# Three convolution tiles moved to TensorE column quarters, and attention's value products turned round

## The chip, the cores and the metric

The kernel runs on one core of one Trainium2 chip. The metric is device time in microseconds, as the median of several executions. One execution was also profiled, and all rows below are of that one.

## The reference, cut to what matters

Two networks follow each other; only the first one (two layers, 512 tokens and 16 meta tokens, so L = 528 rows of width 1024) is touched by the change. Per layer, in float32:

```python
proj = h @ w_in[l]                       # a, g, zc, q, k, v, za, qi, ki, wi
u = a * sigmoid(g)                       # 512 channels
u[t, c] = sum_j w_dw[j, c] * u[t - 30 + j, c] + b_dw[c]     # 31 taps, depthwise
y_conv = silu(layer_norm(u)) * silu(zc)
score = sum_h relu(qi_h . ki) * wi_h     # index scores, causal
keep the 132 best keys per query (top-k)
s = q . k / 8 on the kept keys, 8 heads of 64
p = softmax(s); y_attn = (p @ v) * silu(za)
h = layer_norm(4 ** 0.25 * h + concat(y_conv, y_attn) @ w_out[l])
```

The second network (windowed attention, a gated linear attention, 16 experts, a final gate) starts when the first has ended.

## The kernel before, in words

Activations lie transposed, with channels on the 128 partitions and the 528 (first layer) or 512 (second layer) rows along the free axis. A projection tile (`proj`, the products on L181) makes 128 output channels in 48 recorded passes: eight slices of the contraction, three products of high and low parts (`wh`, `wl`, `hTh`, `hTl`), two pieces of 264 columns. Its weights come in `raw` tiles (three buffers), are split by ScalarE (L159) and VectorE (L160), and its result lies in a PSUM tile of the tag `pp`, which has two buffers.

`p_ag(c)` makes 128 convolution channels: the projections a and g, a tanh (L339), and the product `u` (L340). Then `conv_tap` runs 31 taps over it. For the channel groups in `pconv` (0, 1 and 2 in the first layer, 0 and 1 in the second) ScalarE multiplies by the tap (L323) and GpSimd adds (L325). For the others, group 3 in the first layer and groups 2 and 3 in the second, VectorE does a multiply and add for each tap (L328 and L330). The three tiles of the title are these.

`attn(i)` handles 128 queries: products of queries and keys (L252, L258, two heads at a time in the two row halves of the array), scores plus mask on VectorE into a tile `smb` (L585), the exponential on ScalarE (L590), transposes of the probabilities (L558), copies to SBUF (`pT`, L561), and the value products (L565) with the transposed probabilities as the stationary operand and 64 value columns as the moving one. The rows of a block are then divided by their sums (L505 to L507). In the tail of the layer each block is transposed again (L500) and multiplied by the gate `sza` (L501), and the output projection follows (`pp<-yah,wh` on L181).

The order of issue on each engine is fixed at compile time from priorities, written down as `self.plan`. In the first layer the levels run w, topk, tail, idx, proj, conv, att, ag, rest, fill; in the second w, tail, idx, conv, proj, att, ag, topk, rest, fill. The phases are traced in these orders:

```python
('ag0', 'idx', 'q', 'k', 'sc', 'v', 'ag2', 'ag3', 'topk', 'ag1', 'zc', 'att', 'za')   # first layer
('idx', 'q', 'k', 'sc', 'ag1', 'v', 'ag0', 'ag3', 'topk', 'ag2', 'att', 'za', 'zc')   # second layer
```

A tile is allocated by tag: all tiles of a tag share its buffers (`sb(shape, name, tag, bufs)`). The tag `sm` has two buffers; before the change only `smb` and the gated result in the tail (`yah`, `yal`) use it in the first network. The PSUM tag `s` with four buffers holds every PSUM tile that isn't `pp`. DMAs of weights, and those of `vM` (16 partitions each, from SBUF to SBUF, L481), are issued from SyncE's queue (SPq).

Of the kernel before, what the change touches and what calls it, by code (L numbers as in the profile page):

```python
# [24 lines left out]
W31 = 31  # L25
PAD = W31 - 1
ALPHA = 4.0 ** 0.25
# [41 lines left out]
class Net:  # L69
# [202 lines left out]
    def layer(self, l):  # L272
# [25 lines left out]
        nc.vector.tensor_copy(cvec, pcv)  # L298
        taps = self.sb([128, 4, 31], "taps")
        nc.vector.tensor_scalar(taps, cvec[:, :, 0:31], 0.5, None, op0=ALU.mult)  # L300

# [15 lines left out]
        def conv_tap(c, j):  # L317
            src = u[:, c, j + q0:j + q0 + T]
            if c in pconv:
                if not prod:  # L320
                    prod.append(self.sb([128, 2, L], "prod", "zM"))
                pr = prod[0][:, j % 2, :T] if j else cv[:, c, :]
                nc.scalar.activation(pr, src, AF.Identity, scale=taps[:, c, j:j + 1], bias=0.0 if j else cvec[:, c, 31:32])  # L323
                if j:
                    nc.gpsimd.tensor_tensor(cv[:, c, :], cv[:, c, :], pr, op=ALU.add)  # L325
                return
            if j == 0:
                nc.vector.tensor_scalar(cv[:, c, :], src, taps[:, c, 0:1], cvec[:, c, 31:32], op0=ALU.mult, op1=ALU.add)  # L328
            else:
                nc.vector.scalar_tensor_tensor(cv[:, c, :], src, taps[:, c, j:j + 1], cv[:, c, :], op0=ALU.mult, op1=ALU.add)  # L330

        def p_ag(c):
            self.go("ag")
            ps = []
            for n in ("a", "g"):
                raw = self.load_w(w_in, WCOL[n] + 128 * c, 128)
                ps.append(self.proj(self.split_w(raw), 128, hT, KT, fsegs))
            th = self.sb([128, L], "th", "rl", 3)
            nc.scalar.activation(fseg(th), ps[1], AF.Tanh, scale=0.5)  # L339
            nc.vector.scalar_tensor_tensor(fseg(u[:, c, PAD:]), fseg(th), 1.0, ps[0], op0=ALU.add, op1=ALU.mult)  # L340
            self.go("conv")
            for j in range(W31):
                conv_tap(c, j)
# [75 lines left out]
        def topk_short(i):  # L419
# [5 lines left out]
            m8 = self.sb([128, 8], "m8", bufs=4)  # L425
            v = self.sb([128, 1], "tkv")
            pad = -out % 8
# [64 lines left out]
        def gated(col, r, src):  # L492

            if not gate_ready:
                rows_out.append((col, r, src))
                return
            sza = gate_ready[0]
            pt = self.ps([128, 4, 128], "tp")
            for k in range(4):
                nc.tensor.transpose(pt[:, k, :r], src[:r, k * 128:(k + 1) * 128], self.ident[:r, :r])  # L500
            nc.vector.tensor_mul(sza[:, :, col:col + r], pt[:, :, :r], sza[:, :, col:col + r])  # L501
# [32 lines left out]
        def attn(i):  # L534
# [15 lines left out]
            mxv = mx.rearrange("p (x q) -> p q x", q=2)  # L550
            po = self.ps([128, 8, 64], "po")
            first = [True]

            def pv(p, x0, sm):
                pt = self.ps([128, 4, 128], "tp")
                for x in range(hb):
                    for j in range(i + 1):
                        nc.tensor.transpose(pt[:, x * (i + 1) + j, :], sm[:, x, 128 * j:128 * (j + 1)], self.ident)  # L558
                n = hb * (i + 1)
                pT = self.sb([128, 4, 128], "pT", bufs=4)  # L560
                nc.scalar.copy(pT[:, :n], pt[:, :n])  # L561
                for x in range(hb):
                    h = 2 * (x0 + x) + p
                    for j in range(i + 1):
                        nc.tensor.matmul(po[:, h, :], pT[:, x * (i + 1) + j, :], v[:, j, h * 64:(h + 1) * 64], start=first[0],  # L565
                                         stop=False, skip_group_check=True)
                        first[0] = False

            pend = []
            for x0 in range(0, 4, hb):  # L570
# [4 lines left out]
                for x in range(hb):  # L575
                    for p in (1, 0):
                        b = slice(64 * p, 64 * p + 64)
                        pairs.append(((pss[p][:, x, :], qT[b, x0 + x, qc], kT[b, x0 + x, NM:w]), dict(start=True, stop=True)))
                self.burst(pairs, pss[0][0:1, 0, 0:1])
                for p in range(2):  # L580
                    xs = slice(x0, x0 + hb)
# [6 lines left out]
                    for x in range(hb):  # L588
                        h = 2 * (x0 + x) + p
                        nc.scalar.activation(sm[:, x, :], sm[:, x, :], AF.Exp, bias=mx[:, h:h + 1], scale=0.125,  # L590
                                             accum_out=ssum[:, h:h + 1])
                    pend.append((p, x0, sm))
                yield
                while len(pend) > 2:
                    pv(*pend.pop(0))
# [11 lines left out]
            nc.scalar.copy(pT, pt)  # L607
            nc.tensor.matmul(po.rearrange("p h d -> p (h d)"), pT, vM, start=False, stop=True, skip_group_check=True)
            dst = yas[i // 2][:, i % 2, :]
            normalise(po, ssum, 128, dst)  # L610
            gated(col, 128, dst)
            yield

# [1061 lines left out]
    def first_block(self):  # L1675
# [12 lines left out]
        for i in range(4):  # L1688
            self.transposes_to(*self.hT, NM + 128 * i, z[:, i, :])
        for l in range(2):  # L1690
            self.cur = None
            self.layer(l)
# [26 lines left out]
```

## Time and profile before

| | us |
|---|---|
| median of 3 executions | 1849.26 |
| lowest and highest | 1848.18, 1853.11 |
| the profiled execution, its time | 1850.64 |
| its span in the profile | 1848.8 |
| mean granted TensorE clock | 0.965 |

The profiled execution's time is 1.84 us above its span and 1.38 us above the median. The first layer ends near 400 us, the second near 760; the rest belongs to the second network. The clock is given as a share of 2.4 GHz.

### The profile page before, as it was taken

How to read it: one execution, taken by the hardware profiler on the slowest of the kernel's cores; microseconds unless marked ns; L12 is line 12 of the kernel's file. 1: busy time of each engine (PE TensorE's matmuls, PEld its weight loads, DVE VectorE, ACT ScalarE, POOL GpSimd, SP SyncE). 2: the span in 40 equal slices, each digit the busy share in tenths (PEclk: the TensorE clock that was granted, in tenths of full speed). 3: DMA queues.
4: the chain of work that ended last, by engine and by line, in shares of the span. 5: the costliest groups of instructions: out<-in, count | busy, mean ns of one | idle time of the engine just before them, and what ended most of it. 6: DMA issues, size and time to landing. Idle time of an engine off the chain costs nothing.

```text
span 1848.8 us, 27815 instructions
## 1 busy us (share of the span) xinstructions
PE 1686.7 (91%) x11323; PEld 1342.3 (73%) x11323; DVE 1010.8 (55%) x1947; ACT 765.4 (41%) x1310; POOL 238.0 (13%) x161
## 2 busy tenths in 40 slices
PE   6989989889998899799999999999899988888888
PEld 6989877889997789799888899999533332233246
DVE  3899994666998985775533445543401221012044
ACT  3874656447666554634355444322300000000026
POOL 1620863000068400000000000000000000000000
PEclk9999989999999899899989999999999999999999
DMA  6213111121222112222122248556799999999961
GB/s 194 69 47 93 46 46 46 30 70 59 69 61 79 46 47 81 89 69 91 36 63 75 76 143 288 158 211 230 280 421 421 421 420 421 421 420 421 419 273 46
DMA packets 147104, 323.35 MB, mean 175 GB/s; under 512 B 13034, under 2 KB 102826, under 8 KB 128672
## 3 DMA queue, kind: packets, MB, share of 16 engines
q1 hardware_dynamic: 142112, 310.54, 45.3%
q10 hardware_dynamic: 3856, 7.37, 1.1%
q0 software_dynamic: 1008, 3.67, 0.5%
q8 instruction: 89, 1.46, 0.3%
q14 instruction: 39, 0.32, 0.1%
HBM read 305.22 MB, written 16.25 MB: 174 GB/s over the span
## 4 chain that ended last, share of the span: by engine, by line
PE 58%; DMA 17%; DVE 15%; ACT 6%; issue 3%; POOL 1%; SPq 0%; ACTq 0%; DVEq 0%; POOLq 0%
PE pp L181 36%; PE pp L1571 7%; DMA rawe<-in_w_exp_down 7%; DMA rawe<-in_w_exp_gate 4%; DMA rawe<-in_w_exp_up 4%; DVE cv L330 3%; PE pp L1631 2%; DVE wl L160 2%; POOL cv L325 1%; ACT wh L159 1%; DVE smb L585 1%; PE po L565 1%; DVE acc L414 1%; DMA rawe<-in_w_ple_gate 1%; DVE m L413 1%
## 5 line engine op out<-in xcount | busy, mean ns | idle before, releaser
L325 POOL TENSOR_TENSOR cv<-cv,prod 128x528 f32<-128x528 f32 (+1 forms) x150 | 231.1, 1541 | 393.7 <-ACT prod L323 385.0
L1571 PE MATMUL pp<-rawe,xf 128*64 128x512 f32 x1024 | 247.8, 600 | 12.7 <-DMA rawe<-in_w_exp_gate 8.6
L181 PE MATMUL pp<-hTh,wh 128*128 128x264 f32 (+2 forms) x1056 | 227.4, 296 | 22.9 <-ACT th L339 8.0
L159 ACT CAST wh<-raw 128x1024 fp32r<-128x1024 f32 (+2 forms) x149 | 150.9, 1016 | 229.7 <-PE pp L181 204.0
L181 PE MATMUL pp<-hTl,wh 128*128 128x264 f32 (+2 forms) x1056 | 226.9, 295 | 0.1
L181 PE MATMUL pp<-hTh,wl 128*128 128x264 f32 (+2 forms) x1056 | 224.6, 293 | 0.0
L160 DVE TENSOR_TENSOR wl<-raw,wh 128x1024 fp32r<-128x1024 f32 (+2 forms) x149 | 187.5, 1259 | 65.9 <-ACT wh L159 59.2
L181 PEld LDWEIGHTS pp<-hTh,wh 128*128 128x128 f32 (+1 forms) x1056 | 170.9, 195 | 29.7 <-ACT th L339 9.3
L1571 PEld LDWEIGHTS pp<-rawe,xf 128*64 128x64 f32 x1024 | 76.8, 137 | 158.5 <-issue 131.0
L181 PEld LDWEIGHTS pp<-hTl,wh 128*128 128x128 f32 (+1 forms) x1056 | 170.7, 195 | 7.5 <-issue 6.7
L181 PEld LDWEIGHTS pp<-hTh,wl 128*128 128x128 f32 (+1 forms) x1056 | 169.8, 194 | 2.2 <-issue 1.6
L181 PE MATMUL pp<-xTh,wh 128*128 128x264 f32 (+1 forms) x752 | 156.3, 289 | 2.8 <-ACT op L1000 2.3
L181 PE MATMUL pp<-xTl,wh 128*128 128x264 f32 (+1 forms) x752 | 156.5, 288 | 0.5 <-DVE xTl L1095 0.5
L181 PE MATMUL pp<-xTh,wl 128*128 128x264 f32 (+1 forms) x752 | 155.2, 286 | 0.0
L1571 PE MATMUL pp<-rawe,hid 128*64 128x512 f32 x512 | 127.6, 616 | 18.6 <-DMA rawe<-in_w_exp_down 18.1
L1460 DVE SCALAR_TENSOR_TENSOR Y<-pp,per,Y 128x512 fp32r<-128x512 f32 x16 | 12.0, 749 | 232.7 <-ACT Y L1459 232.7
L1428 POOL DMA_INDIRECT xr<-xrows,slots x7 | 6.7, 958 | 993.2 <-DMA xrows<-zr 699.5
L323 ACT ACTIVATE prod<-u,taps 128x528 f32<-128x528 f32 (+1 forms) x150 | 107.6, 729 | 50.4 <-POOL cv L325 50.0
L181 PEld LDWEIGHTS pp<-xTh,wh 128*128 128x128 f32 (+1 forms) x752 | 116.8, 190 | 4.8 <-ACT op L1000 2.5
L181 PEld LDWEIGHTS pp<-xTl,wh 128*128 128x128 f32 (+1 forms) x752 | 116.2, 189 | 3.1 <-issue 2.2
L181 PEld LDWEIGHTS pp<-xTh,wl 128*128 128x128 f32 (+1 forms) x752 | 116.1, 189 | 0.8 <-issue 0.8
L1571 PEld LDWEIGHTS pp<-rawe,hid 128*64 128x64 f32 x512 | 40.6, 141 | 99.5 <-issue 61.0
(504 smaller groups left out, 2972.1 us busy)
## 6 DMA issues: line engine op xcount, KB each, us to landing
rawe<-in_w_exp_gate SPq DMA_DIRECT2D x53, 1024.0 KB, 16.3
rawe<-in_w_exp_up SPq DMA_DIRECT2D x52, 1024.0 KB, 15.0
rawe<-in_w_exp_down SPq DMA_DIRECT2D x51, 1024.0 KB, 19.6
raw<-in_w_in SPq DMA_DIRECT2D x45, 1024.0 KB, 5.3
rawe<-in_w_exp_down SPq DMA_DIRECT2D x26, 512.0 KB, 15.5
rawe<-in_w_exp_up SPq DMA_DIRECT2D x22, 512.0 KB, 16.2
rawe<-in_w_exp_gate SPq DMA_DIRECT2D x22, 512.0 KB, 17.4
raw<-in_w_in SPq DMA_DIRECT2D x20, 512.0 KB, 6.5
```

The lines of the kernel that those rows point to most:

```text
L159: nc.scalar.copy(wh, raw_view)
L160: nc.vector.tensor_sub(wl, raw_view, wh.bitcast(F32))
L181: nc.tensor.matmul(ps[:m, s, x:min(x + k, n)], a[:, t, :m], b[:, c0 + x:min(c0 + x + k, c1)], start=(t == 0 and pi == 0 and x == 0), stop= ...
L323: nc.scalar.activation(pr, src, AF.Identity, scale=taps[:, c, j:j + 1], bias=0.0 if j else cvec[:, c, 31:32])
L325: nc.gpsimd.tensor_tensor(cv[:, c, :], cv[:, c, :], pr, op=ALU.add)
L330: nc.vector.scalar_tensor_tensor(cv[:, c, :], src, taps[:, c, j:j + 1], cv[:, c, :], op0=ALU.mult, op1=ALU.add)
L413: nc.vector.max(m8, acc)
L414: nc.vector.match_replace(acc, m8, acc, NEG_MARK)
L565: nc.tensor.matmul(po[:, h, :], pT[:, x * (i + 1) + j, :], v[:, j, h * 64:(h + 1) * 64], start=first[0], stop=False, skip_group_check=True)
L585: nc.vector.tensor_tensor_reduce(sm[:, x, :], pss[p][:, x, :], acc[:, NM:w], 1.0, mi[:, h:h + 1], ALU.add, ALU.max, mx[:, h:h + 1])
L1571: nc.tensor.matmul(ps[a, s, :], x[:, a], r, start=(t == 0 and k == 0), stop=(t == KT - 2 and k == 1), skip_group_check=True)
L1631: nc.tensor.matmul(ps[k][:, k, :], a[:, t, :], wp[t][:, w, k * 512:(k + 1) * 512], start=(t == 0 and pi == 0), stop=(t == KT - 1 and pi == 2))
```

## The change

- `taps` gets a leading zero, so that there are 32 taps, and `u` one more column of padding.
- `conv_products(c)` replaces VectorE's taps for the three tiles. Sixteen small products with slices of the identity spread the taps over PSUM, and one VectorE product with `mask32` makes of them 32 diagonal blocks `w` (128 x 32 each). Sixteen DMAs on SyncE's queue copy `u`, 32 channels at a time and shifted by 0 to 3 rows, into two tiles `us` of the tag `sm`. Then 64 products, eight for each of four channel quarters and two halves of the rows, put 32 output channels each on one column quarter of the array, and ScalarE copies the sum with the bias to `cv`.
- In `attn`, the value products have the values as the stationary operand (64 columns, on one column half of the array for each of two heads) and the probabilities as the moving one, so that the result `po` is transposed. The reciprocal sums are brought to that layout by eight products with a broadcast column (`pr`), a ScalarE copy and a VectorE product. The gate is then one VectorE product, without transposes. The product with the meta values `vM` becomes four.
- `mask32` is made once at the start.

```diff
-PAD = W31 - 1
+PAD = W31
+CQ = 4
...
-        taps = self.sb([128, 4, 31], "taps")
-        nc.vector.tensor_scalar(taps, cvec[:, :, 0:31], 0.5, None, op0=ALU.mult)
+        taps = self.sb([128, 4, W31 + 1], "taps")
+        nc.vector.memset(taps[:, :, 0:1], 0.0)
+        nc.vector.tensor_scalar(taps[:, :, 1:], cvec[:, :, 0:31], 0.5, None, op0=ALU.mult)
...
-            if j == 0:
-                nc.vector.tensor_scalar(cv[:, c, :], src, taps[:, c, 0:1], cvec[:, c, 31:32], op0=ALU.mult, op1=ALU.add)
-            else:
-                nc.vector.scalar_tensor_tensor(cv[:, c, :], src, taps[:, c, j:j + 1], cv[:, c, :], op0=ALU.mult, op1=ALU.add)
...
+        def conv_products(c):
+            n = T // 2
+            nx = T + W31 + 1 - CQ
+            pt = self.ps([128, 4, 8], "pcv")
+            for g in range(4):
+                for k in range(CQ):
+                    nc.tensor.matmul(pt[32 * k:32 * k + 32, g, :], self.ident[:, 32 * g:32 * g + 32], taps[:, c, k::CQ], start=True, stop=True)
+            w = self.sb([128, 4, 8, 32], "cwt", "k2l")
+            nc.vector.tensor_tensor(w.rearrange("p g e c -> p (g e) c"), self.mask32[:, None, :].to_broadcast([128, 32, 32]),
+                                    pt.rearrange("p g e -> p (g e)")[:, :, None].to_broadcast([128, 32, 32]), op=ALU.mult)
+            us = [self.sb([128, 2, nx], "us", "sm", 2) for _ in range(2)]
+            for g in range(4):
+                for k in range(CQ):
+                    nc.sync.dma_start(us[g // 2][32 * k:32 * k + 32, g % 2, :], u[32 * g:32 * g + 32, c, k + q0:k + q0 + nx])
+            ps = self.ps([128, 2, 512], "pp", "pp", 2)
+            for k in range(2):
+                products = []
+                for e in range(8):
+                    for g in (3, 2, 1, 0):
+                        x0 = CQ * e + n * k
+                        products.append(((ps[32 * g:32 * g + 32, k, :n], w[:, g, e, :], us[g // 2][:, g % 2, x0:x0 + n]),
+                                         dict(start=e == 0, stop=e == 7, skip_group_check=True)))
+                self.burst(products)
+            nc.scalar.activation(cv[:, c, :].rearrange("p (k n) -> p k n", k=2), ps[:, :, :n], AF.Identity, scale=1.0, bias=cvec[:, c, 31:32])
...
+            if c not in pconv:
+                conv_products(c)
+                return
...
-            po = self.ps([128, 8, 64], "po")
+            po = self.ps([128, 4, 128], "po")
...
+                products = []
                 for x in range(hb):
                     for j in range(i + 1):
-                        nc.tensor.matmul(po[:, h, :], pT[:, x * (i + 1) + j, :], v[:, j, h * 64:(h + 1) * 64], start=first[0],
-                                         stop=False, skip_group_check=True)
+                        for p in (1, 0):
+                            h = 2 * (x0 + x) + p
+                            products.append(((po[64 * p:64 * p + 64, x0 + x, :], v[:, j, h * 64:(h + 1) * 64], pTs[p][:, x * (i + 1) + j, :]),
+                                             dict(start=first[p], stop=False, skip_group_check=True)))
+                self.burst(products)
...
-            nc.tensor.matmul(po.rearrange("p h d -> p (h d)"), pT, vM, start=False, stop=True, skip_group_check=True)
+            for x in range(4):
+                nc.tensor.matmul(po[:, x, :], vM[:, 128 * x:128 * x + 128], pT, start=False, stop=True, skip_group_check=True)
+            rs = self.sb([128, 8], "rs", bufs=2)
+            nc.vector.reciprocal(rs, ssum)
+            nc.vector.tensor_scalar(rs, rs, 0.5, None, op0=ALU.mult)
+            pr = self.ps([128, 4, 128], "tp")
+            self.burst([((pr[64 * (h % 2):64 * (h % 2) + 64, h // 2, :], rs[:, h:h + 1].to_broadcast([128, 64]), self.ident),
+                         dict(start=h < 2, stop=True, skip_group_check=True)) for h in range(8)])
             dst = yas[i // 2][:, i % 2, :]
-            normalise(po, ssum, 128, dst)
-            gated(col, 128, dst)
+            nc.scalar.copy(dst, pr.rearrange("p x q -> p (x q)"))
+            nc.vector.tensor_mul(dst, dst, po.rearrange("p x q -> p (x q)"))
+            gated(col, None, dst)
```

`gated(col, None, dst)` multiplies `dst` into the gate without transposes. `burst` issues its products one behind the other on TensorE.

## Rows read from the trace of the kernel before

**Rows 1.** The page: busy time by engine, and the chain that ended last by line.
```profile
PE 1686.7 (91%) x11323; PEld 1342.3 (73%) x11323; DVE 1010.8 (55%) x1947; ACT 765.4 (41%) x1310; POOL 238.0 (13%) x161
...
PE pp L181 36%; PE pp L1571 7%; DMA rawe<-in_w_exp_down 7%; DMA rawe<-in_w_exp_gate 4%; DMA rawe<-in_w_exp_up 4%; DVE cv L330 3%; PE pp L1631 2%; DVE wl L160 2%; POOL cv L325 1%; ACT wh L159 1%; DVE smb L585 1%; PE po L565 1%; DVE acc L414 1%; DMA rawe<-in_w_ple_gate 1%; DVE m L413 1%
```

**Rows 2.** Stretches: us; busy PE, PEld, DVE, ACT, POOL; PEclk; DMA share; GB/s.
```profile
185.00:327.00 142.00, 127.54 (x908) 113.98 (x908) 113.33 (x248) 90.95 (x181) 89.83 (x58) 0.93 0.14 45
549.00:695.00 146.00, 131.64 (x982) 118.89 (x981) 132.40 (x288) 86.14 (x172) 64.73 (x43) 0.94 0.18 57
...
620.00:630.00 10.00, 5.22 (x29) 4.18 (x28) 10.00 (x20) 1.45 (x2) 4.95 (x4) 0.68 0.00 0
640.00:650.00 10.00, 10.00 (x81) 9.04 (x81) 9.93 (x27) 3.47 (x6) 0.00 (x0) 1.00 0.00 0
```

**Rows 3.** Groups of instructions by form up to 780 us: busy us, mean ns.
```profile
L330 DVE SCALAR_TENSOR_TENSOR cv<-u,taps,cv 128x512 f32<-128x512 f32 x60 | 54.9, 927 | 0.5
L330 DVE SCALAR_TENSOR_TENSOR cv<-u,taps,cv 128x528 f32<-128x528 f32 x30 | 34.7, 1157 | 0.2
```

**Rows 4.** TensorE's groups, 185 to 327 and 549 to 695 us; chain, one tile.
```profile
L181 PE MATMUL pp<-hTl,wh 128*128 128x264 f32 x184 | 41.9, 309 | 0.0
L565 PE MATMUL po<-v,pT 128*128 128x64 f32 x160 | 21.3, 277 | 3.9 <-ACT pT L561 3.9
L558 PE MATMUL tp<-base,smb 128*128 128x128 f32 x80 | 12.3, 277 | 1.1 <-ACT smb L590 0.8
...
L181 PE MATMUL pp<-hTh,wl 128*128 128x264 f32 x204 | 44.8, 297 | 0.0
...
148.90 5.88 PE pp L181 x48
```

**Rows 5.** TensorE in order of time: start, us, line, count.
```profile
196.72 0.50 PE L558 MATMUL tp<-base,smb 128*128 128x128 f32 x3
197.15 0.59 PE L252 MATMUL pidx<-qk 64*128 64x384 f32 x1
...
293.76 1.02 PE L608 MATMUL po<-vM,pT 128*128 128x512 f32 x2
...
681.30 0.72 PE L565 MATMUL po<-v,pT 128*128 128x64 f32 x5
681.86 0.28 PE L605 MATMUL tp<-base,smm 128*128 128x128 f32 x1
...
682.35 0.49 PE L655 MATMUL tp<-base,cv 128*128 128x128 f32 x3
...
1401.50 1.51 PE L1571 MATMUL pp<-rawe,xf 128*64 128x512 f32 x6
```

**Rows 6.** ScalarE and VectorE in order of time: convolution read, products `u`.
```profile
673.40 0.20 ACT L650 ACTIVATE warm<-cv 128x1 f32<-128x1 f32 x1 [3.79 <-DVE cv L330]
...
200.72 0.69 DVE L340 SCALAR_TENSOR_TENSOR u<-th,pp 128x528 f32<-128x528 f32 x1
...
587.60 0.73 DVE L340 SCALAR_TENSOR_TENSOR u<-th,pp 128x528 f32<-128x528 f32 x1
...
615.85 0.69 DVE L340 SCALAR_TENSOR_TENSOR u<-th,pp 128x528 f32<-128x528 f32 x1
```

**Rows 7.** Tiles `smb` and `vM`: duration ns min/median/max, first and last start.
```profile
L585 DVE CUSTOM_DVE_ANT_0 smb<-pidx,acc,mi x64: 339/536/751, 185.2 to 675.1; 128x384 f32<-128x384 f32 x16, 128x128 f32<-128x128 f32 x16, 128x256 f32<-128x256 f32 x16, 128x512 f32<-128x512 f32 x16
...
L481 SPq DMA_DIRECT2D vM<-vm x16: 507/576/625, 148.8 to 548.0; - x16
...
DMA to landing us min/median/max: 1.8/2.2/3.4
```

**Rows 8.** The end of the first layer's attention, and SyncE's queue, in order of time.
```profile
326.67 0.67 DVE L507 TENSOR_TENSOR yas<-po,rs 128x512 f32<-128x512 f32 x1
...
333.12 0.82 PE L181 MATMUL pp<-yah,wh 128*128 128x264 f32 x3 [2.59 <-ACT yah L195]
...
532.57 0.38 SPq L151 DMA_DIRECT2D raw<-in_w_in  x1
```

More of the change, by code (lines that the diff above doesn't have):

```diff
@@ L317, in conv_tap @@
         def conv_tap(c, j):
[L318 to L326, printed above, removed]
@@ L327, in conv_tap @@
-            if j == 0:
-                nc.vector.tensor_scalar(cv[:, c, :], src, taps[:, c, 0:1], cvec[:, c, 31:32], op0=ALU.mult, op1=ALU.add)
-            else:
-                nc.vector.scalar_tensor_tensor(cv[:, c, :], src, taps[:, c, j:j + 1], cv[:, c, :], op0=ALU.mult, op1=ALU.add)
+            src = u[:, c, j + 1 + q0:j + 1 + q0 + T]
+            if not prod:
+                prod.append(self.sb([128, 2, L], "prod", "zM"))
+            pr = prod[0][:, j % 2, :T] if j else cv[:, c, :]
+            nc.scalar.activation(pr, src, AF.Identity, scale=taps[:, c, j + 1:j + 2], bias=0.0 if j else cvec[:, c, 31:32])
@@ new lines, in conv_tap @@
+            if j:
+                nc.gpsimd.tensor_tensor(cv[:, c, :], cv[:, c, :], pr, op=ALU.add)
+        def conv_products(c):
[22 more added lines that the diff above has]
+            nc.scalar.activation(cv[:, c, :].rearrange("p (k n) -> p k n", k=2), ps[:, :, :n], AF.Identity, scale=1.0, bias=cvec[:, c, 31:32])
@@ L425, in topk_short @@
             m8 = self.sb([128, 8], "m8", bufs=4)
-            v = self.sb([128, 1], "tkv")
+            v = self.sb([128, 1], "tkv", "am")
             pad = -out % 8
@@ L497, in gated @@
             sza = gate_ready[0]
+            if r is None:
+                dst = sza[:, :, col:col + 128]
+                nc.vector.tensor_mul(dst, src.rearrange("p (x q) -> p x q", x=4), dst)
+                return
             pt = self.ps([128, 4, 128], "tp")
@@ L550, in attn, with pv @@
             mxv = mx.rearrange("p (x q) -> p q x", q=2)
-            po = self.ps([128, 8, 64], "po")
-            first = [True]
-            def pv(p, x0, sm):
-                pt = self.ps([128, 4, 128], "tp")
+            po = self.ps([128, 4, 128], "po")
+            first = [True, True]
+            def pv(x0, sms):
+                n = hb * (i + 1)
+                pTs = []
+                for p in range(2):
+                    pt = self.ps([128, 4, 128], "tp")
+                    for x in range(hb):
+                        for j in range(i + 1):
+                            nc.tensor.transpose(pt[:, x * (i + 1) + j, :], sms[p][:, x, 128 * j:128 * (j + 1)], self.ident)
+                    pTs.append(self.sb([128, 4, 128], "pT", bufs=4))
+                    nc.scalar.copy(pTs[p][:, :n], pt[:, :n])
+                products = []
                 for x in range(hb):
                     for j in range(i + 1):
[L558 to L564, printed above, removed]
-                        nc.tensor.matmul(po[:, h, :], pT[:, x * (i + 1) + j, :], v[:, j, h * 64:(h + 1) * 64], start=first[0],
-                                         stop=False, skip_group_check=True)
-                        first[0] = False
+                        for p in (1, 0):
+                            h = 2 * (x0 + x) + p
+                            products.append(((po[64 * p:64 * p + 64, x0 + x, :], v[:, j, h * 64:(h + 1) * 64], pTs[p][:, x * (i + 1) + j, :]),
+                                             dict(start=first[p], stop=False, skip_group_check=True)))
+                            first[p] = False
+                self.burst(products)
             pend = []
@@ L579, in attn @@
                 self.burst(pairs, pss[0][0:1, 0, 0:1])
+                sms = []
                 for p in range(2):
@@ L591, in attn @@
                                              accum_out=ssum[:, h:h + 1])
-                    pend.append((p, x0, sm))
+                    sms.append(sm)
+                pend.append((x0, sms))
                 yield
-                while len(pend) > 2:
+                while len(pend) > 1:
                     pv(*pend.pop(0))
@@ L1689, in first_block @@
             self.transposes_to(*self.hT, NM + 128 * i, z[:, i, :])
+        self.mask32 = self.sb([128, 32], "mask32", "xr")
+        nc.vector.tensor_reduce(self.mask32, self.ident.rearrange("p (s c) -> p c s", s=4), axis=AX.X, op=ALU.add)
         for l in range(2):
```

## The prediction

> **What bounds the kernel now.** The page first: TensorE is busy for 91% of the span, and the projections on L181 alone are 36% of the chain that ended last, while VectorE's taps on L330 are 3% of it [rows 1]. So this is a kernel bound by TensorE, with places where another engine holds it up. The table by stretch shows the two places that the change touches: from 185 to 327 us (first layer) and from 549 to 695 us (second). VectorE is busy for 113 of 142 us in the one and 132 of 146 in the other, and there TensorE loses time: at 620 to 630 it is busy for 5.2 of 10 us at a granted clock of 0.68, so partly at 1.2 GHz instead of 2.4, while at 640 to 650 it is busy throughout at 1.00 [rows 2].
>
> How much is lost? I count TensorE's work at its spacing. A projection tile of 48 passes takes 5.88 us [rows 4], 0.1225 each. Five value products span 0.72 us with a last one of about 0.28, so they follow at 0.11 us; two passes of 512 columns span 1.02 us with a last of 0.59, so at 0.43, which is 0.84 ns per column [rows 5]. First layer: 550 projection passes (three groups like the one shown) are 67 us, 160 value products 18, 80 transposes 9 [rows 4], and the rest of attention, counted from the program at the same spacings (64 key passes two at a time about 10 us, eight `vM` passes at 0.43, 70 small ones at 0.11), 21, which cancels in what follows: 115 of 142 us, so 27 lost. Second layer: 13 projection tiles (609 recorded passes [rows 4]) are 76 us, with the same attention 125 of 146, so 21 lost.
>
> **What the change removes.** Ninety L330 instructions, 54.9 and 34.7 us [rows 3], with their three first taps some 92 us of VectorE, 36 in the first layer and 56 in the second. None of it is worth its own length: it is worth what TensorE loses by it, at most the 27 and 21 us.
>
> **What it adds to TensorE.** Each convolution tile has 64 products of two recorded passes (float32 products are recorded in twos: 80 value products of a layer are 160 passes). A pass of 264 columns is 0.22 us. Whether quarters run side by side no row shows; halves do: six passes of the expert products span 1.51 us with a last of 0.59, so three pairs at 0.46, about the 0.43 that one full-array pass of 512 columns takes [rows 5]. By the nearest row I take four side by side: 128 x 0.22 / 4 = 7.1 us. The bounds are 7.1 and, two at a time, 14.2. The 32 small passes that spread the taps are about 1 us, so some 8.6 us a tile with the turns into and out of the mode. VectorE's making of `w` is one product of 1024 columns, about 1.2 us, off the path, since it needs only the taps.
>
> **The value products.** Before, 160 passes at 0.11 are bound by something other than their 64 columns (which would be 0.054). After, 160 passes of 128 columns, 0.107, two at a time: 8.6 us for 17.8, a gain of 9.2 a layer. Gone too are 16 transposes for the gate (2 us). Added are 16 passes a block for the reciprocal sums (3.4 us a layer), and turns between full-array and half-array products: after the last transpose of a row the key products began 0.20 us later instead of 0.11 [rows 5], so 0.1 a turn, 15 bursts, 3 us. Net, 5 us less a layer. ScalarE's four copies of 0.6 us are hidden: it is busy for 91 of 142 us [rows 2]. The four smaller `vM` products cost what the one did.
>
> The Trainium skill (TensorEngine Tiling (Array Packing), Key Properties) says that changing the tiling mode drains TensorE. [...] If each of the 30 turns cost a whole transpose's latency of 0.27 us, an estimate, the layer would lose 8 us instead of 3, and the sum below would be up by 10.
>
> **The wait that it adds.** `us` takes both buffers of the tag `sm`, and in trace order these tiles come ahead of all `smb`. Does that hold attention back? Read the tail: `cv` was complete at 673.40 [rows 6], the tail stands above att in the levels, and yet its first transpose (L655) ran at 682.35, right behind the last attention tile traced before it on the tag `s` (L605, 681.86) [rows 5]. So buffers of a tag are given in trace order. Before, `smb` is first written at 185.2 in the first layer [rows 7] and near the start of the stretch from 549 in the second. After, VectorE's step on `smb` waits until the products of the last `us` are done, in the second layer those of group 2. Behind it queue the exponentials, the transposes and the value products.
>
> When is that? `u` of group 3 in the first layer came at 200.7 [rows 6]; without attention's products among its own, about 193. Then 16 DMAs on SyncE's queue: a load is issued in 0.38 us [rows 8], a small one in 0.58 [rows 7], so 6 to 9 us; I take 7.2, with 2.2 to land [rows 7]. TensorE can do one projection (ag1's a) meanwhile, but the next needs the `pp` buffer of the convolution sum, so it idles some 5 us, and as at 620 to 630 [rows 2], where a third of the clock was gone, what follows runs slower: 3 us more. Products to about 213, then attention, 28 us later than before. SyncE's queue holds loads of weights behind the 16, but those run three buffers ahead.
>
> First layer: 115 - 5 + 8.6 = 118.5 us of work, 9 lost at the landing, 3 elsewhere, makes 130.5 against 142: 11.5 gained, and about 0.5 in the tail, where the transposes ahead of the gate (between 326.7 and 333.1 [rows 8]) go: **12 us**.
>
> Second layer, step by step: ag0's g ends about 553.5, ag3's two projections at 567, `u` 568.5 (before 587.6 [rows 6]), `us` landed 578, products to 588 with the slow clock, ag2's g behind their copy to 595, `u` 596 (before 615.9), za's first tile to 601.5, landed 606, products to 615.5. Left are 7 projection tiles (41 us) and attention (40, with its share of the tail's transposes 42): 698.5 if TensorE is packed as at 640 to 650, against 695. **Lost: 4 us.** Bounds: 12 lost if the old 21 us of gaps stay, 10 gained if attention weren't held (work 135 us of 146).
>
> Sum: -12 + 4 = -8 on the profiled execution's 1850.64, so 1842.6; that execution is 1.4 above the median, so 1841 as a median. The second network only moves.
>
> **The rivals.** (a) *Buffers are given in order of readiness.* Then attention starts as before. First layer 118.5 us of work with 6 lost is 17.5 less, second 10 to 12 less: 28, so **1821**. Against it stands L655 at 682.35.
> (b) *Slower: attention, pressed behind group 2 in the second layer, becomes the bound.* It has 83 us, some 21 a block; before, the four took some 125 us, from the start of the stretch at 549 to `smb`'s last at 675.1 [rows 2, 7], with VectorE full. At 25 us a block the layer ends at 715, 20 later than before: with the first layer's 12, **1857**. It decides from 21 us a block on. For it: in one block each step waits on VectorE, ScalarE and TensorE in turn. Against it: VectorE is nearly free then.
> (c) *Quarters run two at a time*: 7.1 more for each of three tiles, all on TensorE: -8 + 21, **1862**. For it: two passes of one product must follow each other. The Trainium skill (TensorE: Matmul & The Clock Gate, Part 3) states 2.38 times for three column tiles and 3.07 for four row tiles; by the 3.07 a tile is 9.2 us, an estimate, and the sum 1847. No row shows quarters.
> (d) *It does nothing that can be measured*: the second layer keeps its gaps and gives back the first one's gain, -12 + 11: **1848**.
>
> **Chances.** Forecast 0.36, (a) 0.18, (b) 0.14, (c) 0.12, (d) 0.20. A change under 0.3% (5.5 us) can't be told from none. Of the forecast (own range 1833 to 1847) 0.27 are faster and 0.09 same; (a) is faster; (b) and (c) are slower; of (d) 0.14 same, 0.02 faster, 0.04 slower. So faster 0.47, same 0.23, slower 0.30. The range reaches to (a) and (c): 1820 to 1862.
>
> **What would show it.** Right: no L330; the first L585 of the first layer near 213 and of the second near 615; 32-column passes starting four together; value products pairwise at 0.11; the output projection about 12 us earlier in the first layer, and the second layer's own length 4 longer. Wrong: L585 at 185 (then (a)); quarter passes in twos (c); TensorE idle between value products after 615 (b); `us` landing 15 us after `u`, which would add 6 us three times over.

## The result

The change makes the kernel slower: **1877.3 us** median (1875.88 to 1881.06, 4 executions) against 1850.52 (1848.18 to 1853.11, 4) on the same chip, a ratio of 1.0148 with a 95% interval of 1.0125 to 1.017. The forecast was 1841 and its range 1820 to 1862. The profiled execution took 1881.06 us with a span of 1879.3, 30.4 more than before.

Where the time went is best read from the end of each layer's output projection (the last pass on `pp<-ych`): 393.1 and 752.5 us before, 391.3 and 783.1 after. So the first layer is 1.8 shorter instead of 12, and the second, from end to end, takes 391.8 instead of 359.4: 32.4 longer instead of 4. The second network takes as long as before (1096.2 of 1096.3).

### The profile page after: what moved, and what is told of

Its sections match the earlier page's. It is cut to its first block, busy times and chain, and to the rows that moved or that the text cites. A ratio compares the mean times of both kernels' runs of the same rounds, so it can differ in the third digit from the quotient of the medians.

```text
span 1879.3 us, 29068 instructions
## 1 busy us (share of the span) xinstructions
PE 1692.2 (90%) x11947; PEld 1343.8 (72%) x11947; DVE 928.1 (49%) x1860; ACT 773.4 (41%) x1320; POOL 221.1 (12%) x161
## 4 chain that ended last, share of the span: by engine, by line
PE 65%; DMA 15%; DVE 10%; ACT 5%; issue 2%; POOL 1%; SPq 1%; ACTq 0%; DVEq 0%; POOLq 0%
PE pp L182 39%; PE pp L1619 8%; DMA rawe<-in_w_exp_gate 6%; DMA rawe<-in_w_exp_down 5%; DMA rawe<-in_w_exp_up 4%; PE pp L1679 2%; DVE wl L161 2%; POOL cv L327 1%; SPq L344 1%; PE pp L259 1%; DVE acc L441 1%; PE tp L594 1%; PE pidx L253 1%; PE po L253 1%; DVE m L440 1%
## 5 line engine op out<-in xcount | busy, mean ns | idle before, releaser
L327 POOL TENSOR_TENSOR cv<-cv,prod 128x528 f32<-128x528 f32 (+1 forms) x150 | 214.2, 1428 | 396.6 <-ACT prod L325 387.8
L160 ACT CAST wh<-raw 128x1024 fp32r<-128x1024 f32 (+2 forms) x149 | 151.0, 1017 | 241.4 <-PE pp L182 216.0
L182 PE MATMUL pp<-hTh,wh 128*128 128x264 f32 (+2 forms) x1056 | 225.4, 291 | 18.2 <-ACT th L363 7.3
L161 DVE TENSOR_TENSOR wl<-raw,wh 128x1024 fp32r<-128x1024 f32 (+2 forms) x149 | 187.3, 1257 | 91.5 <-ACT wh L160 85.1
L182 PE MATMUL pp<-hTl,wh 128*128 128x264 f32 (+2 forms) x1056 | 220.8, 289 | 0.0
L182 PE MATMUL pp<-hTh,wl 128*128 128x264 f32 (+2 forms) x1056 | 219.7, 287 | 0.0
L182 PEld LDWEIGHTS pp<-hTh,wh 128*128 128x128 f32 (+1 forms) x1056 | 166.7, 190 | 25.7 <-ACT th L363 9.3
L182 PEld LDWEIGHTS pp<-hTl,wh 128*128 128x128 f32 (+1 forms) x1056 | 165.9, 190 | 4.4 <-issue 3.7
L182 PEld LDWEIGHTS pp<-hTh,wl 128*128 128x128 f32 (+1 forms) x1056 | 165.9, 190 | 2.8 <-issue 2.4
L182 PE MATMUL pp<-xTh,wh 128*128 128x264 f32 (+1 forms) x752 | 154.3, 286 | 2.9 <-ACT op L1048 2.3
L182 PE MATMUL pp<-xTl,wh 128*128 128x264 f32 (+1 forms) x752 | 155.8, 286 | 0.8 <-DVE xTl L1143 0.8
L182 PE MATMUL pp<-xTh,wl 128*128 128x264 f32 (+1 forms) x752 | 155.3, 284 | 0.0
L182 PEld LDWEIGHTS pp<-xTh,wh 128*128 128x128 f32 (+1 forms) x752 | 115.7, 190 | 4.6 <-ACT op L1048 2.5
L182 PEld LDWEIGHTS pp<-xTl,wh 128*128 128x128 f32 (+1 forms) x752 | 115.8, 190 | 4.2 <-issue 3.0
L182 PEld LDWEIGHTS pp<-xTh,wl 128*128 128x128 f32 (+1 forms) x752 | 116.0, 190 | 0.8 <-issue 0.8
```

What stands on the lines that cost most here:

```text
L160: nc.scalar.copy(wh, raw_view)
L161: nc.vector.tensor_sub(wl, raw_view, wh.bitcast(F32))
L182: nc.tensor.matmul(ps[:m, s, x:min(x + k, n)], a[:, t, :m], b[:, c0 + x:min(c0 + x + k, c1)], start=(t == 0 and pi == 0 and x == 0), stop= ...
```

## The profile after

The page: VectorE's taps are gone from the chain, and the DMAs of L344 (`us`) and the products of L259 have come into it.

```profile
PE 1692.2 (90%) x11947; PEld 1343.8 (72%) x11947; DVE 928.1 (49%) x1860; ACT 773.4 (41%) x1320; POOL 221.1 (12%) x161
...
PE pp L182 39%; PE pp L1619 8%; DMA rawe<-in_w_exp_gate 6%; DMA rawe<-in_w_exp_down 5%; DMA rawe<-in_w_exp_up 4%; PE pp L1679 2%; DVE wl L161 2%; POOL cv L327 1%; SPq L344 1%; PE pp L259 1%; DVE acc L441 1%; PE tp L594 1%; PE pidx L253 1%; PE po L253 1%; DVE m L440 1%
```

The table by stretch, to be laid beside [rows 2] (columns as there). VectorE's load has fallen from 113 to 83 us and from 132 to 63, but TensorE is busy for less of the second stretch (110.66 for 131.64), and there are whole slices in which VectorE stands still and TensorE nearly so (580 to 590 and 620 to 630). Behind the last products, from attention's first score to its last (the last line), it is full again.

```profile
185.00:327.00 142.00, 125.27 (x1124) 110.56 (x1123) 83.13 (x224) 95.22 (x188) 79.31 (x58) 0.94 0.18 54
549.00:695.00 146.00, 110.66 (x1044) 101.15 (x1043) 62.63 (x168) 69.68 (x136) 57.29 (x42) 0.88 0.24 70
...
580.00:590.00 10.00, 0.81 (x8) 0.73 (x12) 0.00 (x0) 5.13 (x8) 9.45 (x8) 0.50 0.41 96
...
620.00:630.00 10.00, 3.34 (x37) 3.01 (x41) 0.00 (x0) 0.00 (x0) 0.00 (x0) 0.53 0.30 71
640.00:650.00 10.00, 10.00 (x86) 8.66 (x84) 3.23 (x9) 5.96 (x16) 0.00 (x0) 1.00 0.33 107
...
635.20:718.10 82.90, 82.12 (x736) 73.04 (x737) 42.15 (x143) 45.03 (x110) 0.00 (x0) 1.00 0.16 52
```

What TensorE waits for stands in its timeline: in brackets the idle time and what ended it. Three waits, 15.45, 17.90 and 14.39 us, stand ahead of the three tiles' first products. (The first bears the name of ScalarE's `prod`; what it coincides with is the last transfer of `us`, issued at 209.8 and landed 2.0 later.)

```profile
196.20 0.40 PE L182 MATMUL pp<-hTh,wl 128*128 128x264 f32 x2
212.04 0.62 PE L253 MATMUL pp<-us,cwt 128*32 128x264 f32 x1 [15.45 <-ACT prod L325]
...
212.69 5.32 PE L259 MATMUL pp<-us,cwt 128*32 128x264 f32 x59
217.70 0.39 PE L253 MATMUL pp<-us,cwt 128*32 128x264 f32 x1
...
221.50 0.51 PE L182 MATMUL pp<-hTh,wh 128*128 128x264 f32 x2
...
589.19 0.61 PE L253 MATMUL pp<-us,cwt 128*32 128x256 f32 x1 [17.90 <-DMA us<-u]
...
626.66 0.60 PE L253 MATMUL pp<-us,cwt 128*32 128x256 f32 x1 [14.39 <-DMA us<-u]
```

Two more things are in these lines. The half tile that runs right behind the wait takes 5.66 us (212.04 to 217.70), the second half 3.80: the granted clock was 0.62 in the one and 1.00 in the other, and 0.50, the lower of the two levels, in the stretch 580 to 590, idle but for its end. And the next projection (L182) starts at 221.50, only behind the products, though its weights had been split by 198.7 us (L160, L161): TensorE did nothing in the wait.

SyncE's queue shows the transfers, sixteen to a line, 10.0 us from the start of the first issue to the end of the last:

```profile
200.37 10.01 SPq L344 DMA_DIRECT2D us<-u  x16
...
577.53 10.01 SPq L344 DMA_DIRECT2D us<-u  x16
...
615.06 10.00 SPq L344 DMA_DIRECT2D us<-u  x16
```

VectorE in order of time: `u` of the second layer's tiles, and the first score of a layer, written into `smb` (L624 is L585 of before). Both layers' attention begins when the last product of a tile is done, 36 us later than before in the first layer (185.2 [rows 7]).

```profile
221.58 0.62 DVE L624 CUSTOM_DVE_ANT_0 smb<-pidx,acc,mi 128x384 f32<-128x384 f32 x1 [8.37 <-PE pp L259]
...
576.78 0.69 DVE L364 SCALAR_TENSOR_TENSOR u<-th,pp 128x528 f32<-128x528 f32 x1
...
614.29 0.70 DVE L364 SCALAR_TENSOR_TENSOR u<-th,pp 128x528 f32<-128x528 f32 x1
635.19 0.62 DVE L624 CUSTOM_DVE_ANT_0 smb<-pidx,acc,mi 128x384 f32<-128x384 f32 x1 [20.21 <-PE pp L259]
```

And the last score of the second layer starts at 717.3 (tile `smb`); the projections were done at 711.2, but the output projection has to wait for attention's tail until 728.98.

```profile
L624 DVE CUSTOM_DVE_ANT_0 smb<-pidx,acc,mi x64: 339/547/755, 221.6 to 717.3; 128x384 f32<-128x384 f32 x16, 128x128 f32<-128x128 f32 x16, 128x256 f32<-128x256 f32 x16, 128x512 f32<-128x512 f32 x16
...
728.98 0.73 PE L182 MATMUL pp<-yah,wh 128*128 128x264 f32 x4 [2.21 <-ACT yah L196]
```

The value products in the first layer's last block. Sixteen passes of 128 columns start at 320.74 and the next work at 321.76: 1.02 us, where sixteen of 64 columns would take 1.76 at the spacing of 0.11 from [rows 5]. The smaller `vM` products take 1.09 (to 322.85), about the 1.02 of before [rows 5].

```profile
320.74 0.32 PE L253 MATMUL po<-pT,v 128*64 128x128 f32 x1
...
320.91 0.93 PE L259 MATMUL po<-pT,v 128*64 128x128 f32 x13
321.76 1.16 PE L649 MATMUL po<-pT,vM 128*128 128x128 f32 x8
322.85 0.32 PE L253 MATMUL tp<-base,rs 128*64 128x128 f32 x1
```

## The experiments

The theory after the result: the tiles' waits for `us`, and attention held back by `us` in its buffers, make the loss. The rivals: the turned value products are slow; or the waits alone count; or the tiles' own work does. All runs were timed against the kernel before (its median was 1847.95 to 1849.35 in these). In the table, "layer 1" and "layer 2" are the ends of the output projections in the profiled execution, "scores" the first score of the second layer's attention, and "rest" what the span has behind layer 2. They are of one execution each, so kernels with the same code in a layer show how far such a time can be read: the first layer ends at 379.5, 380.3 and 378.8 in e5, e8 and e11, at 393.5 and 391.3 in e4 and e7; the second, from end to end, takes 350.8 in e9 and 356.2 in e11, both with the old values in it.

| kernel | median us | ratio (95%) | layer 1 | scores | layer 2 | rest |
|---|---|---|---|---|---|---|
| before | | | 393.1 | 551.8 | 752.5 | 1096.3 |
| after | 1877.3 | 1.0148 (1.0125 to 1.017) | 391.3 | 635.2 | 783.1 | 1096.2 |
| e1 convolution part alone | 1900.45 | 1.0266 (1.0231 to 1.0302) | 396.0 | 641.6 | 797.5 | 1103.3 |
| e2 value part alone | 1859.89 | 1.007 (1.0048 to 1.0092) | 389.7 | 548.4 | 752.5 | 1105.6 |
| e3 `us` elsewhere | 1858.2 | 1.0039 (1.0018 to 1.0061) | 388.0 | 547.1 | 758.4 | 1098.0 |
| e4 products later | 1871.39 | 1.0121 (1.0097 to 1.0144) | 393.5 | 629.7 | 777.0 | 1093.2 |
| e5 both of these | 1843.82 | 0.9968 (0.9956 to 0.998) | 379.5 | 541.8 | 741.8 | 1097.9 |
| e6 two queues | 1874.02 | 1.0135 (1.0118 to 1.0152) | 393.9 | 628.0 | 775.9 | 1095.8 |
| e7 later, tiles early | 1857.3 | 1.0048 (1.0031 to 1.0065) | 391.3 | 603.9 | 760.9 | 1093.8 |
| e8 e7, `us` elsewhere | 1837.16 | 0.9932 (0.9916 to 0.9949) | 380.3 | 553.8 | 734.2 | 1100.4 |
| e9 e8, old values | 1850.03 | 0.9996 (0.9982 to 1.001) | 384.8 | 558.4 | 735.6 | 1110.2 |
| e10 e8, two queues | 1851.29 | 1.0015 (0.9999 to 1.003) | 385.5 | 564.2 | 749.4 | 1102.8 |
| e11 e8, values in layer 1 | 1847.93 | 0.9993 (0.9983 to 1.0004) | 378.8 | 556.3 | 735.0 | 1113.8 |

### The two parts alone

e1 is the kernel after without the diff's pieces in `attn` and `gated`; e2 is the kernel before with those pieces alone.

> The convolution part alone; the value products as before the change. Theory (the loss is the wait of the three convolution tiles for `us` and the hold that `us` puts on attention): about 1885 us (1878 to 1892), that is the changed kernel's 1877 plus the 5 us a layer that the turned value products were forecast to save, less what of it was hidden. Rival (the turned value products are slow, by their turns between array modes and the longer chain of a block): 1850 to 1865, below the changed kernel.

> The turned value products alone; the taps on VectorE as before the change. Theory: 1838 to 1848 us, 2 to 12 below the kernel before, since 9 us of value products a layer become shorter while VectorE's taps still hold some of it up. Rival (turned value products cost): 1855 to 1875.

e1 took 1900.45, slower than theory and rival. e2 took 1859.89, the rival's side, so the value part seemed to cost. The table says otherwise: at the end of layer 2 e2 stands at 752.5, just where the kernel before does, and its whole loss is in the second network, which the change does not touch. There SyncE's queue holds the experts' weights. It waits for a product (the buffer of a load) longer than before; the waits of that queue, before and e2 (line, what ended it, us in all, times, longest):

```profile
SPq L1509 <- PE pp L1571: 15.4, 2, 12.8
```

```profile
SPq L1530 <- PE pp L1592: 18.9, 1, 18.9
```

All runs fall into two groups by it: where the longest such wait is 12.6 to 15.3 us (before, after, e3 to e8), the rest takes 1093 to 1100; where it is 18.9 to 24.1 (e1, e2, e9, e10, e11), it takes 1103 to 1114. Behind it lie some 400 us with the DMA engines full (420 GB/s), in which nothing is caught up. The wait need not be all of it: the first load of the experts is issued 377 to 386 us behind the end of layer 2, a spread of 9 us of its own. Why an edit in the first network moves either is open: the order of issue written at compile time may do it, but no run shows that, and one compiled kernel varies as well (of the ten executions of e3 four took 1849 to 1851 us and six 1858 to 1862). So the profiled executions of these five carry 6 to 18 us in a stage that their edit does not touch, and the layers' ends are what to compare.

By those, the value part gains 3.4 in layer 1 and loses 3.4 in layer 2 by itself; beside the convolution part it gains 4.7 and 9.7 (after against e1). The 3.4 of layer 2 is less than the 5.4 between e9 and e11. The convolution part, not the values, makes the loss: layer 2 ends 45 later in e1.

### The hold, and the waits

e3 puts `us` into the buffer of the index queries (free between the scores and the gate). To make room, the taps lie in the tile of `mask32` and a small tile of the second network in another tag.

```diff
-            us = [self.sb([128, 2, nx], "us", "sm", 2) for _ in range(2)]
+            big = self.sb([128, 4, nx], "us", "qi")
+            us = [big[:, 0:2], big[:, 2:4]]
```

> The changed kernel, with `us` in the buffer that lies idle between the index queries and the gate, so that `smb` waits for no convolution product; nothing is left out. Theory: the 18 us between the last projection of the second layer and its output projection go, and attention's products fill part of the three waits of 15.5, 17.9 and 14 us: 1835 to 1860 us; the first attention product of the first layer comes near 185 instead of 221. Rival (the waits alone make the loss, and attention is not the bound): 1870 to 1880, the waits of the same length.

e4 leaves `us` where it is and moves the sums behind the next two projection tiles (the next `p_ag`, or the first two tiles of za or zc).

```diff
-            ps = self.ps([128, 2, 512], "pp", "pp", 2)
...
+            def sums():
+                ps = self.ps([128, 2, 512], "pp", "pp", 2)
...
+            while late:
+                late.pop(0)()
             self.go("conv")
             if c not in pconv:
-                conv_products(c)
+                late.append(conv_products(c))
```

> The changed kernel, with a convolution tile's products behind the next two projection tiles in the program, so that those fill the wait for `us`; `us` stays in attention's buffers. Theory: TensorE has no gap over 6 us ahead of the products, some 35 of the 47 us come back, and attention, held some 10 us longer in the second layer, takes 10 to 20 again: 1848 to 1866 us. Rival (attention held behind `us` is all of the loss): 1880 to 1890, since attention starts later still.

e3 is as the theory said: scores start where they did before, at 184.9 and 547.1, and 24.7 of the 30.6 us at the end of layer 2 come back. It does not undo the hold alone, for attention's products now run in the waits: from the first issue of `us` to the products TensorE stands still for 2.9, 2.3 and 5.7 us, for 11.7, 11.7 and 11.6 in the kernel after. What it does there it does at a clock of 0.53 to 0.57 (the column before the last two). Tile `smb` and these stretches of e3:

```profile
L625 DVE CUSTOM_DVE_ANT_0 smb<-pidx,acc,mi x64: 343/534/751, 184.9 to 660.4; 128x384 f32<-128x384 f32 x16, 128x128 f32<-128x128 f32 x16, 128x256 f32<-128x256 f32 x16, 128x512 f32<-128x512 f32 x16
...
202.22:217.77 15.55, 12.62 (x68) 9.43 (x68) 15.55 (x47) 12.24 (x26) 14.34 (x11) 0.53 0.31 73
576.39:589.74 13.35, 11.05 (x69) 9.11 (x69) 4.73 (x14) 9.49 (x20) 10.97 (x10) 0.53 0.36 84
617.88:629.61 11.73, 5.99 (x34) 4.93 (x34) 4.57 (x25) 5.83 (x21) 0.00 (x0) 0.57 0.40 95
```

e4 is a miss for the theory's size. The waits did go: TensorE waits 15.5 us for `us` in three times, not 48 (the lines of tile `us`, who waits for what). But only 6.1 us come back at the end of layer 2, because attention is still held, until 629.7, and now the time stands at the end: the projections are done by 685.0 and TensorE is left with attention alone, at a clock of 0.80 and 0.52 (stretches of e4).

```profile
  DMA us<-u: 15.5, 3
...
  DVE smb L632: 17.6, 2
...
690.00:700.00 10.00, 6.52 (x36) 4.74 (x38) 5.41 (x23) 4.04 (x10) 0.00 (x0) 0.80 0.00 0
700.00:710.00 10.00, 10.00 (x40) 4.51 (x38) 2.21 (x8) 2.60 (x6) 0.00 (x0) 0.52 0.00 0
...
629.70:711.30 81.60, 77.39 (x641) 64.84 (x642) 38.58 (x139) 41.98 (x106) 0.00 (x0) 0.92 0.12 40
```

In after, e4 and e6 layer 2 ends 147 to 148 us behind the first score, wherever TensorE's waits are (156 and 157 in e1, with the old values, and in e7, with the tiles early). But not for one reason: in after eight projection tiles are left at the first score and TensorE is busy for 82.1 of the 82.9 us to the last, at full clock; in e4, where six are left, it is busy for 77.4 of 81.6 at a clock of 0.92. What e4 puts into the waits it takes from the end, where attention then takes as long without it. Attention takes 83 us from the first score to the last in the kernel after (635.2 to 718.1), 10.9 more to the output projection, and that takes 54.

e5 does both (and traces zc ahead of za in layer 2).

> `us` in the idle buffer and the products behind the next two projection tiles, together; in the second layer zc is traced ahead of za so that the gate's buffer is free in time; nothing is left out. Theory (the hold on attention is most of the loss, and the waits cost only as far as nothing else can fill them): the second layer's output projection ends at 752 to 758 us, as with `us` elsewhere alone (758.4) or a little earlier, and the whole takes 1845 to 1857 us. Rival (the waits of TensorE are a loss of their own that adds to the hold): the two gains add up, 20 and 6 us off the changed kernel, the projection ends near 750 and the whole takes 1838 to 1848.

The rival's time holds: 41.3 us come back, more than the 24.7 and 6.1 together. In layer 2 by itself the gains add up: from end to end it takes 21.3 us less than after in e3, 8.3 less in e4 and 29.5 less in e5 (with zc and za exchanged, which no run takes apart). What is more than the sum is layer 1's: 3.3 us less in e3, 2.2 more in e4, 11.8 less in e5. From 150 us to that layer's end TensorE stands still for 16.5 us in e3, at a clock of 0.94; in e5, where two projections stand ahead of the products as well, for 13.4 at 0.97. In e4 attention is held still longer, to 226.3 us.

### One queue or two

```diff
-                    nc.sync.dma_start(us[g // 2][32 * k:32 * k + 32, g % 2, :], u[32 * g:32 * g + 32, c, k + q0:k + q0 + nx])
+                    (nc.scalar if k % 2 else nc.sync).dma_start(us[g // 2][32 * k:32 * k + 32, g % 2, :], u[32 * g:32 * g + 32, c, k + q0:k + q0 + nx])
```

> The changed kernel with every second of the 16 DMAs issued on ScalarE's queue. Theory: the issue of 10 us becomes 5, attention is freed 5 us earlier after the first and 10 to 15 earlier after the last tile, since the three tiles stand in a row: the second layer's output projection ends at 766 to 775 (changed kernel 783.1), the whole 1862 to 1871. Rival (the transfers, not their issue, set the wait): no change, 1873 to 1880.

A miss: 1874.02, the rival's number, though not its reason. In the first layer the products came at 210.9 instead of 212.0. ScalarE's queue shows why: its share went out one by one between the taps that ScalarE makes at GpSimd's pace, 1.38 us apart, so that half the transfers took 9.0 us to issue. In the second layer the waits were 1.4 and 4.4 us shorter.

```profile
201.11 0.73 ACT L325 ACTIVATE prod<-u,taps 128x528 f32<-128x528 f32 x1 [0.65 <-POOL cv L327]
201.12 0.51 ACTq L344 DMA_DIRECT2D us<-u  x1
202.49 0.73 ACT L325 ACTIVATE prod<-u,taps 128x528 f32<-128x528 f32 x1 [0.65 <-POOL cv L327]
202.50 0.51 ACTq L344 DMA_DIRECT2D us<-u  x1
```

### The tiles ahead of attention

e7 is e4 with the second layer's tiles traced early; e8 adds `us` elsewhere, as in e3.

```diff
-             ('idx', 'q', 'k', 'sc', 'ag1', 'v', 'ag0', 'ag3', 'topk', 'ag2', 'att', 'za', 'zc'),
+             ('idx', 'q', 'k', 'sc', 'ag1', 'ag3', 'v', 'ag2', 'ag0', 'topk', 'att', 'za', 'zc'),
```

> The products behind the next two projection tiles as in the earlier run, and in the second layer the two tiles that go by products come before the one that goes over ScalarE and GpSimd (order 1, 3, 2, 0 and no longer 1, 0, 3, 2), so that `us` gives attention's buffers back before attention could start; `us` stays in those buffers. Theory (the hold is the loss): the second layer's output projection ends at 750 to 762, as with `us` elsewhere, the whole 1845 to 1862. Rival (something else in the second layer, as the products' own work or attention's longer blocks): 770 and later, 1865 to 1875.

> The run with the tiles early, and `us` in the idle buffer as well. Theory: no hold at all and no wait, 745 to 755 for the end of the second layer's output projection, the whole 1838 to 1850. Rival (once attention is not held, TensorE's added work of the tiles, 8.6 us each, is what is left): 755 to 762, 1850 to 1858.

e7 brings the scores from 629.7 to 603.9 and the end of layer 2 from 777.0 to 760.9: that fits the hold, though the new order moves other phases too. e8, with no hold, is faster than both kernels: **1837.16 us, 0.9932** of before. Layer 2 ends at 734.2, lower than even the theory's 745; the second network takes 4 us more than before. TensorE now lacks work for 9 us of the first stretch and 8 of the second, against 14.5 and 14.4 [rows 2], at a clock of 0.98 and 0.99 against 0.93 and 0.94:

```profile
185.00:327.00 142.00, 132.99 (x1184) 114.89 (x1183) 92.93 (x245) 102.24 (x201) 79.12 (x58) 0.98 0.18 54
549.00:695.00 146.00, 138.19 (x1319) 118.29 (x1320) 76.95 (x206) 90.28 (x183) 44.34 (x34) 0.99 0.19 57
```

Its timeline shows a tile at full clock: half a tile, 64 passes, from 221.47 to 225.16, 0.058 us a pass.

```profile
221.47 0.41 PE L253 MATMUL pp<-us,cwt 128*32 128x264 f32 x1
...
221.72 3.51 PE L259 MATMUL pp<-us,cwt 128*32 128x264 f32 x59
225.16 0.37 PE L253 MATMUL pidx<-qk 64*128 64x128 f32 x1
```

### What is left on e8

e9 is e8 with the old value products, e10 e8 with two queues, e11 e8 with turned values in the first layer alone.

> The run with the tiles early and `us` elsewhere, with the value products as before the change. It sizes the value part where nothing else holds attention up. Theory (turned value products save 5 us a layer wherever TensorE is the bound): 6 to 12 us slower than the run with both, 1843 to 1850. Rival (they only look shorter, and attention's chain with its added sums and wider bursts takes it back, as the value part alone took 3 us more in the second layer): within 3 us of the run with both, 1834 to 1840.

> The run with the tiles early and `us` elsewhere, with every second of the 16 DMAs on ScalarE's queue. Theory (the wait for `us` is now filled by two projection tiles, so that the 10 us of issue cost nothing): no change, 1834 to 1840. Rival (the issue still delays the products, or the loads of weights behind it): 1828 to 1833.

> The run with the tiles early and `us` elsewhere, with the turned value products in the first layer alone; the second layer's value products are as before the change. In the two pairs of runs where nothing held attention, turned values shortened the first layer by 3.4 and 4.5 us and lengthened the second by 3.4 and 3.1. Theory (that is a property of the second layer, where the products shorten nothing that attention waits for): the first layer's output projection ends at 380 to 381, the second's at 730 to 732, 3 us before the run with both layers turned. Rival (the 3 us come from the order in which the instructions happen to be laid out, and go with any edit): the second layer's own length within 1.5 us of 353.9 or longer. The whole would be 1833 to 1838 by both, unless the experts' weight loads in the second block come later, as they did in four of the runs, which takes 6 to 14 us more.

e9's median agrees with the theory, but for the wrong reason: its layers end at 384.8 and 735.6, 4.5 and 1.4 later than in e8, and of the 11.2 us between the two spans 9.8 are the second network's. So the turned values are worth 4.5 us in layer 1 and cost 3.1 in layer 2 (350.8 from end to end against 353.9). e11 was to tell whether that cost is one of layer 2. It isn't: with old values there, layer 2 takes 356.2, longer than e8's 353.9. The rival holds: e9 and e11 have the same second layer, 5.4 us apart, so that what the value part does there (from 3.4 longer to 2.3 shorter where attention is free) is unsettled.

e10 is a miss for both: slower by 5.2 us in layer 1 and 10.0 in layer 2 (363.9 against 353.9). The scores of layer 2 start 10.4 us later, of which 5.2 are layer 1's. ScalarE's queue carries 24 issues of 0.58 us beside attention's exponentials and copies; that this delays them was not shown by a run of its own.

## Why the prediction was wrong

The wait was foreseen, and its place: `us` before `smb`, tag `sm` in trace order, attention behind the last tile's products. That was right, as e3 shows, and rival (a) falls. So was the length of attention behind it: 83 us forecast, 82.9 measured, with TensorE full as assumed. That the numbers meet so closely is luck, for eight projection tiles were left for it and not seven. What failed is when it starts, and what follows it.

**"TensorE can do one projection meanwhile."** It did none. The products had been put into its queue ahead of that projection, and TensorE ran it only behind them, at 221.50; with the products behind two projections (e4) the three waits together fall from 48 us to 15.5. The forecast left 5 us idle; 15.45, 17.90 and 14.39 were measured. After the second tile of the three, the two projections for the next (12 us) then stood between the products and the next `u`, 14.9 us instead of the 8 forecast.

**"16 DMAs in 7.2 us."** They took 10.0, 0.59 each and 0.63 from one to the next: the 0.58 of the small copies [rows 7] was the nearer row, not the 0.38 of a weight load, and the result lies outside the bounds of 6 to 9. Landing was 2.0 for 2.2. From `u` to the first product it was 12.4 us each time, for 9.4 to 10.

**The second layer's sum.** Forecast products to 615.5, measured 635.1: `u` of group 3 came 8.3 later than forecast (its projections ended at 571.3 for 567, and behind its tanh it stood 3.6 more, while VectorE finished the mask and split a weight), the two waits add 5.3, the missing projection 6.9, and the products themselves, slow clock included, are 0.8 shorter. These are 20. Then the forecast had attention done at 698.5 and the layer 3.5 longer, so the output projection, at 697.9 before, at 701.4, 2.9 us behind; 10.9 lie between the last score and it in the trace, 8 more. (The eighth projection tile, 5.9 us of TensorE, which the forecast had run in the last wait, is part of the work behind the products here.) Together they are the 28 that the second layer is off.

**The first layer's.** `u` at 199.65 (forecast 193: it took 7.7 off for attention's products, and 1.1 came off), first score at 221.58 (213), and the output projection 8.8 later than forecast: the 8.6 us of the start come out at the end nearly one for one. With 1.4 in the output projection itself that is the other 10 us at the layer's end.

**Rival (b)** had the right side, slower by the second layer, but a wrong reason: attention was not the bound behind group 2, where TensorE is full to the last score, and its blocks don't take 25 us (they take 20.7); they start 20 us later. It was priced at 1857.

**What TensorE lost.** 27 and 21 us were read as recoverable. Of [rows 2] the stretches had 14.5 and 14.4 us without a product; the clock, at 0.93 and 0.94 of full over them, is worth at most 9.9 and 8.8 more, which leaves some 3 of the 27 without a source. The best kernel here recovers 12.8 us in layer 1, tile work included, and 5.5 in layer 2; rival (a), with 17.5 and 10 to 12, asked too much even of a kernel without the hold.

**Two sums** of the forecast don't add up: the first layer's loss at the landing is 5 and 3, so 8 and not 9, and the work of the second layer without the hold is 125 - 5 + 17, so 137 and not 135. Neither would move the forecast by more than 2 us.

**Right**: four quarters side by side. At 0.058 us a pass against the 0.22 worked out for one alone, 3.8 run at a time, and a tile is 7.4 us for the forecast 7.1; rival (c) falls. The 3.07 that the Trainium skill (TensorE: Matmul & The Clock Gate, Part 3) gives for four row tiles would have made 9.2, an estimate; the trace here says 7.4. The value products are as forecast: sixteen passes in 1.02 us are eight pairs at 0.107 and 0.16 for the turns; the Trainium skill's drain on a change of mode (TensorEngine Tiling (Array Packing), Key Properties) costs here no more than that. The sum of the value part was 5 a layer; measured are 3.4 to 4.7 in layer 1 (e2, e9, e1), and in layer 2 nothing that could be settled where attention is free.

## What to carry to other kernels

Here the wait for a new transfer was filled only by work that stood ahead of its user in the same engine's queue (48 us of waits became 15.5 when two projections did); look where the order of issue puts the consumer before counting on what "could run meanwhile". A scratch tile in a shared tag delayed every later tile of that tag (first scores 36 and 83 us later): place it in a buffer that is idle at that time, and produce it before the other users need theirs. Undo two suspected faults together, not only one by one (in layer 1 neither edit alone gave more than 3.3 us, both gave 11.8; in layer 2 they added up), and compare stage by stage: five of these kernels carried 6 to 18 us from a stage that the edit did not touch. See how far apart the same code lies in two kernels before reading a difference of 3 us.

## What the runs showed that was not expected

- An issue on SyncE of a copy of 32 partitions from SBUF to SBUF costs 0.59 us, and sixteen of them 10.0, as much as the products that they feed (7.1 to 10.2). On ScalarE the median is 0.55 and 0.58 (e6, e10), and beside taps 1.38 us apart they went out one by one between them.
- After a wait of 14 to 18 us TensorE is at the lower clock (0.50 in the stretch 580 to 590), and the first half of a tile takes 5.66 us for the second's 3.80. Filling the wait with attention's products alone left it at 0.53 to 0.57 (e3).
- The second network took 6 to 18 us more in the five kernels where a wait of the experts' queue had grown from 12.8 to 18.9 us and more; that the wait is the cause is not shown.
